# Weight tiles whose high part lies 192 bytes further on, modulo 256, than their low part

## The chip, the core and the metric

One core of a Trainium2 chip runs the program. The metric is the device time of one execution in microseconds; the time before is a median of three runs. TensorE multiplies, VectorE (DVE), ScalarE (ACT) and GpSimd (POOL) prepare operands and take results away, and DMA queues bring the weights in from HBM.

## The reference

A decoder trunk of two layers on 512 tokens of width 1024, in float32. Each layer has a SwiGLU network at half weight, a token mixer (retention in the first layer, forgetting attention in the second), a second SwiGLU network, and a gated per-layer input:

```python
h = h + 0.5 * swiglu(rmsnorm(h, nw[0]), ffn_w_in[i, 0], ffn_w_out[i, 0])
hn = rmsnorm(h, nw[1])
h = h + retention(hn, ...)            # layer 0; forgetting_attention in layer 1
h = h + 0.5 * swiglu(rmsnorm(h, nw[2]), ffn_w_in[i, 1], ffn_w_out[i, 1])
gate = jax.nn.sigmoid(rmsnorm(h, nw[3]) @ ple_w_gate[i])
h = h + gate * (p[i] @ ple_w_proj[i])
```

The inner width of the four SwiGLU networks is 2816. A final RMSNorm ends the trunk.

## The kernel before

All work is on tiles of 128 partitions. Activations are kept transposed: a `unit` is a tile of 128 features by 512 tokens, 2048 bytes in each partition.

**High and low parts.** Every operand of a matmul is kept as two float32r numbers, a rounded high part and the low rest. `split` makes them: ScalarE casts the raw tile into the high part (L83), and VectorE or GpSimd subtracts the high part from the raw tile for the low one (L84). In some stages GpSimd's queue adds the raw tile to its negative by an accumulating DMA instead (`negated`, L125 to L127). A product is then three matmuls: high weights with high activations, high weights with low activations, low weights with high activations. So two matmuls in three load a slice of the high part, 128 columns or 512 bytes of it, as the stationary operand.

**Weights.** `Weights` holds one list of 1024-column sources in the order in which TensorE uses them. `chunk`, `first` and `emit_parts` take a tile `wraw` for the DMA and a tile `w8` (shown as `w` in the profile) of 8192 bytes for the two parts: the high part in its first half, the low part in its second. The pool has three such tiles. In the last stage the pool is replaced by another of five (`wkept`), which also lies elsewhere.

**SwiGLU networks.** The first two blocks of the inner width are done by `plain` (L543), in matmuls of 256 columns of activations, in the order high-high, high-low, low-high. The other 20 blocks of each network go by a scheme of seven products per block (`one`, `two`, `three`), each `product` (L508) being twelve matmuls of 256 columns: first eight with the high part of the weights, each slice twice, then four with the low part. Two of the seven take their weights from the pool's tile; the other five from sums of weights that VectorE makes in tiles of the network's own pool (`s12`, `s34`, shown as `s`, and `a12`, shown as `a`). The second matrix is applied in three pieces by `out_blocks`, through `mm3` (L323 to L325) with 512 columns of activations.

**Mixers and gates.** `proj`, `out_part` and `OutBoth` use `mm3` with 512 columns as well; `v_part` (L702 to L704) has the activations stationary and 512 columns of the weights moving. The first layer's gate (`ple`) runs on 512 columns; the second's, the last stage, in two halves of 256, partly from the five kept tiles.

**Order.** TensorE's instructions run in the order written; the other engines' order is a scheduler's. A tile's wait for its reader (a DMA for a free `wraw`, ScalarE for a free `w`) follows from the pools' sizes.

**Places.** The allocation of the built program gives each tile's first byte in its partition. Units begin at 34,336 and then every 2048 bytes, `wraw` at 124,448, `w` at 140,832, 149,024 and 157,216: all leave 32 when divided by 256. Behind them come `tmp` and the small tiles of `stat`; the latter add 192 modulo 256, so that the networks' `sums`, `s` and `a12`, and the last stage's kept `w`, begin at 184,032 and leave 224. Slices are multiples of 512 bytes, and the halves of a unit 1024 bytes apart, so a slice leaves what its tile does; the low parts lie 2048, 4096 or 8192 bytes behind the high ones and leave the same as them.

Of the kernel before, what the change touches and what calls it, by code (L numbers as in the profile page):

```python
# [12 lines left out]
F32R = mybir.dt.float32r  # L13
# [4 lines left out]
P = 128  # L18
# [36 lines left out]
class Weights:  # L55
# [18 lines left out]
    def load(self, src):  # L74
        raw = self.raw_pool.tile([P, 1024], F32, name="wraw")
        self.nc.sync.dma_start(out=raw[:, : src.shape[1]], in_=src)
        return raw

    def split(self, raw, hi, lo, src=None):
        if self.low is None and src is not None:  # L80
            self.negated(raw, hi, lo, src)
            return
        self.nc.scalar.copy(hi, raw)  # L83
        self.low.tensor_tensor(out=lo, in0=raw, in1=hi.bitcast(F32), op=ALU.subtract)  # L84

    def chunk(self, src):
        n = src.shape[1]
        raw = self.load(src)
        if id(src) in self.placed:
            hi, lo = (t.rearrange("p a c -> p (a c)") for t in self.placed.pop(id(src))())  # L90
            self.split(raw, hi, lo)
            return hi, lo
        if self.spare:
            tiles = [self.spare.pop(0)() for _ in range(4)]
            for i in range(2):
                self.split(raw[:, 512 * i : 512 * (i + 1)], tiles[i], tiles[2 + i])
            return Halves(tiles[0:2]), Halves(tiles[2:4])
        t = self.pool.tile([P, 2, 1024], F32R, name="w8")
        self.split(raw[:, :n], t[:, 0, :n], t[:, 1, :n], src)
        return t[:, 0, :], t[:, 1, :]  # L100

    def emit_parts(self, parts):

        nc = self.nc
        halves = lambda ap: ap.rearrange("p (h c) -> p h c", h=2)
        tiles = [
            (
                self.raw_pool.tile([P, 1024], F32, name="wraw"),
                self.pool.tile([P, 2, 1024], F32R, name="w8"),
            )  # L110
            for _ in range(2)
        ]
        for j0, j1 in parts:
            cs = slice(j0 * P, j1 * P)
            for src, (raw, t) in zip(self.plan, tiles):
                r, hi, lo = (halves(x)[:, :, cs] for x in (raw, t[:, 0, :], t[:, 1, :]))
                nc.sync.dma_start(out=r, in_=halves(src)[:, :, cs])
                nc.vector.tensor_copy(hi, r)
                nc.vector.tensor_tensor(out=lo, in0=r, in1=hi.bitcast(F32), op=ALU.subtract)
            yield  # L120
        self.ready += [(t[:, 0, :], t[:, 1, :]) for _, t in tiles]

    def negated(self, raw, hi, lo, src):

# [4 lines left out]
    def first(self, pair):  # L129

        pair.raw = self.load(pair.q)
        pair.t = self.pool.tile([P, 2, 1024], F32R, name="w8")
        hi, lo = pair.t[:, 0, :], pair.t[:, 1, :]
        if pair.direct:
            self.split(pair.raw, hi, lo)
        else:
            self.negated(pair.raw, hi, lo, pair.q)
# [61 lines left out]
def trunk(ctx, tc, a):  # L199
# [110 lines left out]
    def split(src, hi, lo, scale=None):  # L310

        if scale is None:
            high = nc.scalar.copy(hi, src)
            low = nc.vector.tensor_tensor(out=lo, in0=src, in1=hi.bitcast(F32), op=ALU.subtract)  # L314
        else:
            high = nc.scalar.activation(hi, src, AF.Identity, scale=scale)
            low = nc.vector.scalar_tensor_tensor(
                out=lo, in0=src, scalar=scale, in1=hi.bitcast(F32), op0=ALU.mult, op1=ALU.subtract
            )
        return high, low  # L320

    def mm3(out, wh, wl, xh, xl, first, last):
        nc.tensor.matmul(out, wh, xh, start=first, stop=False)  # L323
        nc.tensor.matmul(out, wh, xl, start=False, stop=False)  # L324
        nc.tensor.matmul(out, wl, xh, start=False, stop=last)  # L325

    def halved(acc):
        hi, lo = temp(F32R), temp(F32R)
        split(acc, hi, lo)
        return hi, lo  # L330
# [13 lines left out]
    class Norm:  # L344
# [9 lines left out]
        def halves(self, b):  # L354
            if self.forms is not None:
                return self.quarters(b)
            hi, lo = self.unit(), self.unit()
            split(h[b], hi, lo, self.gain[:, b : b + 1])
            self.hi.append(hi)
            self.lo.append(lo)  # L360

        def plain(self, b):

            g = self.gain[:, b : b + 1]
            if b % 2:
                hi, lo = self.unit(), self.unit()
                split(h[b], hi, lo, g)
                both = [(hi[:, c], lo[:, c]) for c in HALVES]
            else:
                both = []  # L370
                for i, c in enumerate(HALVES):
                    u = self.unit() if i == 0 else unit(ud)
                    both.append(tuple(u[:, d] for d in HALVES))
                    split(h[b][:, c], *both[i], g)
            n = 1 + b % 2
            if n == 1:
                self.forms.append({})
            self.forms[b // 2].update({f"b{n}1": both[0], f"b{n}2": both[1]})
# [126 lines left out]
    def product(out, w, c, forms, name, first=False):  # L505

        xs = [form[name] for form in forms]
        add = lambda w, x, start, stop: nc.tensor.matmul(  # L508
            out, w, x, start=start, stop=stop, skip_group_check=True
        )  # L510
        for j, (xh, xl) in enumerate(xs):
            wh = w[:, 0, c + j * P : c + (j + 1) * P]
            add(wh, xh, first and j == 0, False)
            add(wh, xl, False, False)
        for j, (xh, xl) in enumerate(xs):
            add(w[:, 1, c + j * P : c + (j + 1) * P], xh, False, j == 3)

    def ffn(i, n, nxt, stack, apool, meanwhile=None):

# [32 lines left out]
        def one(m):  # L552
            pair, g, u = live[m]
            product(g[:, c0], pair.t, 0, n.forms, "b11", True)
            product(g[:, c1], pair.s[0], 0, n.forms, "t1")

        def two(m):
            pair, g, u = live[m]
            product(u[:, c1], pair.s[1], 0, n.forms, "t2", True)
            cc = temp()  # L560
            nc.scalar.copy(cc, g)
            nc.vector.tensor_tensor(out=u[:, c1], in0=u[:, c1], in1=cc[:, c0], op=ALU.add)
            u2 = temp()[:, c0]
            nc.scalar.copy(u2, u[:, c1])
            nc.vector.tensor_tensor(out=g[:, c1], in0=g[:, c1], in1=u2, op=ALU.add)  # L565
            live[m] += (cc,)
# [96 lines left out]
    class OutBoth:  # L663
# [5 lines left out]
        def add(self, i, m):  # L669
            srcs, yhi, ylo = self.parts[i]  # L670
            if (i, m // 2) not in self.ws:
                self.ws[i, m // 2] = W.take(srcs[m // 2])
            wh, wl = self.ws[i, m // 2]
            for k in range(4):
                ks = slice((4 * (m % 2) + k) * P, (4 * (m % 2) + k + 1) * P)
                mm3(self.banks[m], wh[:, ks], wl[:, ks], yhi[k], ylo[k], i == 0 and k == 0, i == 1 and k == 3)
# [560 lines left out]
    norms[4].early = True  # L1237
    first = W.emit_parts(((0, 1), (1, 2), (2, 4)))
    next(first)
    load_x(1, 2)  # L1240
    load_x(2, 4)
# [132 lines left out]
```

## Time and profile before

| | |
|---|---|
| median of three runs (lowest to highest) | 2192.59 us (2189.26 to 2194.67) |
| the profiled execution | 2193.35 us |
| its span, first to last instruction | 2191.5 us |
| instructions | 34,456, of them 13,525 matmuls |
| TensorE busy, weight loads busy | 2142.5 us (98%), 1927.9 us (88%) |
| VectorE, ScalarE, GpSimd busy | 1454.5, 1202.4, 472.6 us |
| read from HBM | 262.71 MB, 121 GB/s over the span |
| granted TensorE clock, mean | 0.994 |

In the profile's rows, PE is TensorE's matmul, PEld its weight load, which runs beside the matmul ahead of it. A group's row has line, engine, operation, output and inputs by name, the shapes and the count, then the group's busy time in microseconds, the mean nanoseconds of one, and the idle time ahead of it with what ended it. A timeline row begins with the start and the length in microseconds; neighbours that are alike are merged, with their count. A matmul's recorded length includes its way through the array, so the cost of one in a stream is the distance from its start to the next one's start.

### The profile page before, as it was taken

To read this page: it belongs to the slowest core of one execution; us is meant where nothing else is said; L and a number is where in the kernel's file an instruction comes from. 1 tells how busy PE (TensorE), PEld (TensorE's weight loads), DVE (VectorE), ACT (ScalarE), POOL (GpSimd) and SP (SyncE) were. 2 spreads that over 40 slices of the span, in tenths; PEclk is the share of its full clock that TensorE was granted. 3 is DMA by queue.
4 is the path that set the end of the run, shared out by engine and by line. 5 is a ranking of instruction groups with operands and counts; after the bars stand their busy time and mean duration, and the time that the engine had idled before them with its cause. 6 is when DMAs were issued, how large, how long until landed. Compare 5 with 4: busy or idle time off the path is not lost.

```text
span 2191.5 us, 34456 instructions
## 1 busy us (share of the span) xinstructions
PE 2142.5 (98%) x13525; PEld 1927.9 (88%) x13525; DVE 1454.5 (66%) x2629; ACT 1202.4 (55%) x2027; POOL 472.6 (22%) x354
## 2 busy tenths in 40 slices
PE   8999999999999999999998999999999999999997
PEld 7999997888888798989988999898788899999987
DVE  8686766352533677767758687775675696777765
ACT  7465553433333574745556556464787774655544
POOL 0010003444344000101142011012334200100055
PEclk9999999999999999999999999999999999999999
DMA  5465562222222244746523555463622144654631
GB/s 174 124 167 148 140 164 97 82 95 77 94 77 87 77 128 132 177 119 152 144 94 97 129 160 149 137 167 105 152 81 88 67 125 114 161 154 139 155 106 40
DMA packets 85315, 267.08 MB, mean 122 GB/s; under 512 B 9360, under 2 KB 12944, under 8 KB 85152
## 3 DMA queue, kind: packets, MB, share of 16 engines
q1 hardware_dynamic: 63328, 209.78, 28.2%
q0 software_dynamic: 20592, 54.01, 14.6%
q8 instruction: 106, 1.74, 0.3%
q10 hardware_dynamic: 1232, 1.09, 0.1%
q14 instruction: 57, 0.47, 0.1%
HBM read 262.71 MB, written 2.13 MB: 121 GB/s over the span
## 4 chain that ended last, share of the span: by engine, by line
PE 85%; DVE 6%; ACT 4%; DMA 2%; issue 2%; POOL 1%; SPq 0%; ACTq 0%; DVEq 0%; POOLq 0%
PE bank L508 33%; PE bank L325 14%; PE bank L323 14%; PE bank L324 13%; PE bank L543 4%; PE bank L703 2%; PE bank L702 2%; PE bank L704 2%; DMA wraw<-in_ffn_w_in 1%; ACT p L1006 1%; DVE w L84 1%; ACT p L1008 1%; ACT w L83 1%; DVE tlo L314 1%; PE bank L337 0%
## 5 line engine op out<-in xcount | busy, mean ns | idle before, releaser
L83 ACT CAST w<-wraw 128x1024 fp32r<-128x1024 f32 (+1 forms) x240 | 243.4, 1021 | 420.0 <-PE bank L325 254.9
L325 PE MATMUL bank<-unit_a,w 128*128 128x512 f32 x736 | 287.2, 390 | 4.3 <-DVE w L84 2.6
L323 PE MATMUL bank<-unit_a,w 128*128 128x512 f32 x736 | 288.5, 392 | 1.9 <-ACT w L83 1.6
L324 PE MATMUL bank<-unit_a,w 128*128 128x512 f32 x736 | 286.7, 390 | 0.2 <-DVE unit_a L314 0.2
L84 POOL TENSOR_TENSOR w<-wraw,w 128x1024 fp32r<-128x1024 f32 x93 | 226.8, 2442 | 259.3 <-ACT w L83 246.8
L83 ACT CAST s<-sums 128x512 fp32r<-128x512 f32 x320 | 191.8, 617 | 153.4 <-DVE sums L157 107.4
L325 PE MATMUL bank<-unit_d,w 128*128 128x512 f32 (+1 forms) x712 | 268.2, 377 | 4.6 <-DVE w L84 4.6
L323 PE MATMUL bank<-unit_d,w 128*128 128x512 f32 (+1 forms) x712 | 269.3, 378 | 3.2 <-ACT w L83 1.6
L324 PE MATMUL bank<-unit_d,w 128*128 128x512 f32 (+1 forms) x712 | 268.0, 376 | 1.8 <-DVE unit_d L314 1.8
L84 DVE TENSOR_TENSOR s<-sums,s 128x512 fp32r<-128x512 f32 x320 | 214.1, 685 | 75.8 <-ACT s L83 75.3
L127 POOL DMA_DIRECT2D a<-in_ffn_w_in x80 | 70.3, 878 | 643.4 <-ACT a L126 422.0
L84 DVE TENSOR_TENSOR w<-wraw,w 128x1024 fp32r<-128x1024 f32 (+1 forms) x147 | 173.3, 1184 | 19.5 <-ACT w L83 19.3
L508 PE MATMUL bank<-unit_b,s 128*128 128x256 f32 x880 | 184.4, 276 | 0.7 <-DVE bank L565 0.7
L508 PE MATMUL bank<-unit_d,s 128*128 128x256 f32 x1140 | 178.4, 276 | 0.0
L508 PE MATMUL bank<-unit_a,s 128*128 128x256 f32 x1260 | 175.0, 276 | 1.4 <-ACT unit_a L387 0.9
L604 DVE SCALAR_TENSOR_TENSOR tmp<-bank,rows 128x512 f32<-128x512 f32 x96 | 66.0, 689 | 164.9 <-PE bank L325 163.7
L325 PEld LDWEIGHTS bank<-unit_a,w 128*128 128x128 f32 x736 | 138.1, 188 | 35.5 <-DVE w L84 4.3
L323 PEld LDWEIGHTS bank<-unit_a,w 128*128 128x128 f32 x736 | 138.2, 188 | 32.2 <-ACT w L83 3.5
L324 PEld LDWEIGHTS bank<-unit_a,w 128*128 128x128 f32 x736 | 138.2, 188 | 28.5 <-DVE unit_a L314 0.5
L325 PEld LDWEIGHTS bank<-unit_d,w 128*128 128x128 f32 x712 | 134.3, 189 | 30.7 <-DVE w L84 6.6
L323 PEld LDWEIGHTS bank<-unit_d,w 128*128 128x128 f32 x712 | 134.4, 189 | 30.2 <-ACT w L83 3.3
L508 PEld LDWEIGHTS bank<-unit_a,s 128*128 128x128 f32 x1260 | 158.0, 188 | 1.8 <-ACT unit_a L387 1.1
(292 smaller groups left out, 4787.9 us busy)
## 6 DMA issues: line engine op xcount, KB each, us to landing
wraw<-in_ffn_w_in SPq DMA_DIRECT2D x174, 512.0 KB, 4.3
wraw<-in_ffn_w_out SPq DMA_DIRECT2D x64, 512.0 KB, 4.7
w<-in_ffn_w_in POOLq DMA_DIRECT2D x56, 512.0 KB, 5.4
a<-in_ffn_w_in POOLq DMA_DIRECT2D x80, 256.0 KB, 6.3
wraw<-in_ffn_w_out SPq DMA_DIRECT2D x32, 384.0 KB, 3.7
wraw<-in_ret_qk SPq DMA_DIRECT2D x16, 512.0 KB, 3.5
wraw<-in_ret_v SPq DMA_DIRECT2D x16, 512.0 KB, 3.6
wraw<-in_ret_g SPq DMA_DIRECT2D x16, 512.0 KB, 3.5
```

Of the source, the lines that this page charges most:

```text
L83: self.nc.scalar.copy(hi, raw)
L84: self.low.tensor_tensor(out=lo, in0=raw, in1=hi.bitcast(F32), op=ALU.subtract)
L127: self.nc.gpsimd.dma_start(out=lo, in_=src, accum_op=ALU.add)
L323: nc.tensor.matmul(out, wh, xh, start=first, stop=False)
L324: nc.tensor.matmul(out, wh, xl, start=False, stop=False)
L325: nc.tensor.matmul(out, wl, xh, start=False, stop=last)
L508: add = lambda w, x, start, stop: nc.tensor.matmul(out, w, x, start=start, stop=stop, skip_group_check=True)
L543: nc.tensor.matmul(o[:, HALVES[t]], x[:, ks], y, start=k == t == q == 0, stop=k == KB - 1 and q == 2, skip_group_check=True,)
L604: nc.vector.scalar_tensor_tensor(out=t1, in0=o, scalar=-0.5, in1=n.r, op0=ALU.mult, op1=ALU.mult)
L702: nc.tensor.matmul(os[t], xh, wh[:, js], start=k == 0, stop=False)
L703: nc.tensor.matmul(os[t], xh, wl[:, js], start=False, stop=False)
L704: nc.tensor.matmul(os[t], xl, wh[:, js], start=False, stop=k == KB - 1)
```

## The change

All tiles of the weight pool come from one function. It makes them 2112 elements long, 8448 bytes, which is 256 more; the high part begins 192 bytes into the tile, the low part 4352 bytes into it, a multiple of 256. The high part therefore leaves 224 modulo 256 and the low part 32. In the last stage's kept tiles, which begin at 224, the high part leaves 160 and the low part 224. The three tiles together are 768 bytes longer, so that all that lies behind them keeps what it leaves modulo 256. The users of the tile take the two parts as a pair in place of a three-dimensional tile; `product` accepts both. No instruction, DMA or wait is added or removed.

```diff
+    def wide(self, src):
+
+        at = 48
+        t = self.pool.tile([P, 2112], F32R, name="w8")
+        return t[:, at : at + 1024], t[:, at + 1040 :]
+
...
-        t = self.pool.tile([P, 2, 1024], F32R, name="w8")
-        self.split(raw[:, :n], t[:, 0, :n], t[:, 1, :n], src)
-        return t[:, 0, :], t[:, 1, :]
+        hi, lo = self.wide(src)
+        self.split(raw[:, :n], hi[:, :n], lo[:, :n], src)
+        return hi, lo
...
-                self.pool.tile([P, 2, 1024], F32R, name="w8"),
+                *self.wide(src),
...
-        pair.t = self.pool.tile([P, 2, 1024], F32R, name="w8")
-        hi, lo = pair.t[:, 0, :], pair.t[:, 1, :]
+        pair.t = hi, lo = self.wide(pair.q)
...
+        both = w if isinstance(w, tuple) else (w[:, 0, :], w[:, 1, :])
...
-            wh = w[:, 0, c + j * P : c + (j + 1) * P]
+            wh = both[0][:, c + j * P : c + (j + 1) * P]
...
-            add(w[:, 1, c + j * P : c + (j + 1) * P], xh, False, j == 3)
+            add(both[1][:, c + j * P : c + (j + 1) * P], xh, False, j == 3)
```

More of the change, by code (lines that the diff above doesn't have):

```diff
@@ L108, in emit_parts @@
                 self.raw_pool.tile([P, 1024], F32, name="wraw"),
-                self.pool.tile([P, 2, 1024], F32R, name="w8"),
+                *self.wide(src),
             )
-            for _ in range(2)
+            for src in self.plan[:2]
         ]
@@ L114, in emit_parts @@
             cs = slice(j0 * P, j1 * P)
-            for src, (raw, t) in zip(self.plan, tiles):
-                r, hi, lo = (halves(x)[:, :, cs] for x in (raw, t[:, 0, :], t[:, 1, :]))
+            for src, (raw, wh, wl) in zip(self.plan, tiles):
+                r, hi, lo = (halves(x)[:, :, cs] for x in (raw, wh, wl))
                 nc.sync.dma_start(out=r, in_=halves(src)[:, :, cs])
@@ L120, in emit_parts @@
             yield
-        self.ready += [(t[:, 0, :], t[:, 1, :]) for _, t in tiles]
+        self.ready += [(wh, wl) for _, wh, wl in tiles]
     def negated(self, raw, hi, lo, src):
```

## The prediction, made before the change was run

> **What bounds the kernel now.** I read the page first (busy times, chain), then the groups of TensorE by shape, then TensorE's own timeline in four stretches, because the change moves bytes and nothing else.
>
> ```profile
> span 2191.5 us, 34456 instructions
> PE 2142.5 (98%) x13525; PEld 1927.9 (88%) x13525; DVE 1454.5 (66%) x2629; ACT 1202.4 (55%) x2027; POOL 472.6 (22%) x354
> PE 85%; DVE 6%; ACT 4%; DMA 2%; issue 2%; POOL 1%; SPq 0%; ACTq 0%; DVEq 0%; POOLq 0%
> ```
>
> TensorE is busy for 98% of the span and carries 85% of the chain that ended last. So a nanosecond on each matmul is what counts, and a slot of another engine is not. The groups by shape (mean ns of one is the last figure ahead of the second bar):
>
> ```profile
> L323 PE MATMUL bank<-unit_a,w 128*128 128x512 f32 x736 | 288.5, 392 | 1.9 <-ACT w L83 1.6 <-DVE tmp L1040 0.3
> L323 PE MATMUL bank<-unit_d,w 128*128 128x512 f32 x616 | 241.9, 393 | 3.2 <-ACT w L83 1.6 <-DVE unit_b L317 0.6 <-ACT unit_d L313 0.5
> L508 PE MATMUL bank<-unit_a,s 128*128 128x256 f32 x1260 | 175.0, 276 | 1.4 <-ACT unit_a L387 0.9 <-DVE unit_a L388 0.4
> L508 PE MATMUL bank<-unit_b,w 128*128 128x256 f32 x720 | 132.1, 283 | 0.4 <-ACT tmp L564 0.3
> L508 PE MATMUL bank<-unit_a,w 128*128 128x256 f32 x540 | 80.3, 283 | 1.7 <-ACT tmp L564 1.7
> L323 PEld LDWEIGHTS bank<-unit_a,w 128*128 128x128 f32 x736 | 138.2, 188 | 32.2 <-ACT w L83 3.5
> ```
>
> One product, one shape, two prices: 283 ns with weights from `w`, 276 from `s`. The two kinds of tile differ in place. By the allocation, the units and `w` begin at bytes that leave 32 modulo 256, `s`, `sums` and `a12` at 224, since the small tiles of `stat` between them add 192. The timeline has what counts, start to start:
>
> ```profile
> 138.27 1.52 PE L508 MATMUL bank<-unit_a,s 128*128 128x256 f32 x12
> 139.63 0.73 PE L508 MATMUL bank<-unit_b,a 128*128 128x256 f32 x5
> ...
> 140.99 0.88 PE L508 MATMUL bank<-unit_b,w 128*128 128x256 f32 x6
> ...
> 142.43 0.39 PE L508 MATMUL bank<-unit_a,s 128*128 128x256 f32 x2
> ```
>
> Twelve products from `s` take 139.63-138.27 = 1.36 us, 113.3 ns each; twelve from `w` 142.43-140.99 = 1.44 us, 120.0 ns. So 6.7 ns go where weights and moving operand sit equally modulo 256. The wide matmuls, all on `w` at 32:
>
> ```profile
> 1165.11 0.39 PE L323 MATMUL bank<-unit_a,w 128*128 128x512 f32 x1
> ...
> 1168.96 0.39 PE L325 MATMUL bank<-unit_c,w 128*128 128x512 f32 x1
> 1169.18 0.75 PE L543 MATMUL bank<-unit_b,s 128*128 128x256 f32 x5
> ...
> 1171.66 0.52 PE L543 MATMUL bank<-unit_d,s 128*128 128x256 f32 x3
> ```
>
> The seventeen steps of the first pair give 3.85/17 = 226.5 ns, twice 113.3: for 512 columns it streams as fast, per column, as the good case for 256. The second pair is a warning. It is a `plain` block whose weights lie in `s` tiles, at 224, straight after a wide stretch: 21 matmuls in 2.48 us, 118.1 ns, not 113.3. Place alone does not settle the price; how one got there counts too. The last stage, where five `w` tiles are in a pool of their own at 224, has both:
>
> ```profile
> 2138.60 0.28 PE L323 MATMUL bank<-unit_d,w 128*128 128x256 f32 x1
> ...
> 2140.37 0.28 PE L323 MATMUL bank<-unit_c,w 128*128 128x256 f32 x1
> 2163.43 0.28 PE L323 MATMUL bank<-unit_d,w 128*128 128x256 f32 x1
> ...
> 2165.02 0.28 PE L325 MATMUL bank<-unit_d,w 128*128 128x256 f32 x1
> ```
>
> 15 steps in 1.77 us are 118.0 ns; 14 in 1.59 are 113.6, and that stretch directly follows matmuls with weights at 32. I call these the bad and the good state of weights at 224.
>
> **The change, part by part.** Instructions, DMAs, queues and waits stay as they are. The three tiles grow by 768 bytes together, three times 256, so nothing behind them moves modulo 256. The high part goes from 32 to 224; the low part stays at 32. In the kept pool, high goes from 224 to 160, low stays at 224.
>
> (a) *Products from `w`* (L508): 4 networks x 20 blocks x 2 products x 12 = 1920, of which 8 in 12 load the high part: 1280 x 6.7 = 8.5 us less. Bounds: the full 8.5, or, in the bad state, 1280 x 2.0 = 2.6. I take the good one, for in each block these products stand among `s` products, which run in it.
>
> (b) *`plain` and the narrow gates.* Two loads in three are high.
>
> ```profile
> L543 PE MATMUL bank<-unit_b,w 128*128 128x256 f32 x220 | 35.6, 302 | 3.0 <-DVE w L84 1.4 <-DVE w L119 1.1 <-DVE unit_b L317 0.4
> L543 PE MATMUL bank<-unit_d,w 128*128 128x256 f32 x204 | 30.7, 297 | 0.0
> L543 PE MATMUL bank<-unit_a,w 128*128 128x256 f32 x144 | 20.4, 284 | 0.0
> L543 PE MATMUL bank<-unit_c,w 128*128 128x256 f32 x104 | 16.4, 287 | 0.0
> ```
>
> 672 matmuls, 448 high: between 448 x 2.0 = 0.9 us (as at 1169 us, the same line) and 3.0. Nearest is the same line's 118.1, with a low part at 32 in every third, which favours the good state: I take 2.0 us. The gates' kept tiles go to 160, which no row shows: some 160 matmuls at 113.3 to 120, from 1.1 us more to 0.7 less. I take nothing.
>
> (c) *Wide matmuls* (L323 to L325): 736+616 = 1352 triples, 2704 with high weights, and six calls of 96 in `v_part`, where `w` moves and the units are loaded. No row has wide matmuls with weights at 224. Below: 6.7 ns less each, 18.1 us. Above: 4.7 more (118.0-113.3) on all 4056, 19.1 us. I take zero: a load is recorded with 188 ns and has 226.5 to hide in against 113.3, and 226.5 is already the good rate per column. `v_part` likewise zero, within 576 x 4.7 = 2.7 either way.
>
> (d) *Writers.* ScalarE, VectorE and GpSimd write or read the high part at its new place. VectorE pays 684 ns where its inputs lie at 224 and 32, and 686 where both lie at 32:
>
> ```profile
> L157 DVE TENSOR_TENSOR sums<-wraw 128x512 f32<-128x512 f32 x160 | 109.6, 686 | 55.7 <-DMA wraw<-in_ffn_w_in 55.3
> L157 DVE TENSOR_TENSOR sums<-sums,wraw 128x512 f32<-128x512 f32 x160 | 109.4, 684 | 0.8
> L84 POOL TENSOR_TENSOR w<-wraw,w 128x1024 fp32r<-128x1024 f32 x93 | 226.8, 2442 | 259.3 <-ACT w L83 246.8 <-issue 11.9
> L84 POOL TENSOR_TENSOR s<-wraw,s 128x1024 fp32r<-128x1024 f32 x1 | 2.9, 2886 | 0.0
> ```
>
> A subtraction of GpSimd with its high part at 224 took 2886 ns against a mean of 2442 at 32. If that is the place, 93 x 0.44 = 41 us more on an engine that is idle 78% of the span. I cost it at nothing; with that cover gone it would show as TensorE waiting for `w` L84 on POOL.
>
> Sum: 8.5+2.0 = 10.5 us less on TensorE, which is idle only 49 us; the next engine is at 66%, so I let it through in full. The profiled execution took 2193.35 us (span 2191.5, 1.85 around it), 0.8 above the median of the runs, 2192.59. It becomes 2182.9, and the median 2182.1.
>
> **The Trainium skill beside the rows.** 6.7 ns between two places of the same operand, above, are not what the Trainium skill says ("TensorE: Matmul & The Clock Gate", section "Step-by-step: what each phase is for"): by it, weight loads and the moving operand have independent read ports and loading the next weights takes no read bandwidth from the running matmul. By that rule the sum would be nought, 2192.6; the trace disagrees by 6.7 ns in 120. The same page ("Back-to-back issue gap") puts isolated matmuls at columns/2.4 + 2.5 ns, 215.8 for 512. The trace has 226.5; by the page 10.7 ns could still go from each wide matmul, an estimate of 29 us over the 2704, which speaks for rival 2.
>
> **Rivals.** (1) *Wide matmuls pay* (the other side). After `s` products the wide stretch does not start at its good rate:
>
> ```profile
> 87.47 0.40 PE L323 MATMUL bank<-unit_d,w 128*128 128x512 f32 x1
> ...
> 88.63 0.39 PE L325 MATMUL bank<-unit_d,w 128*128 128x512 f32 x1
> ...
> 90.44 0.39 PE L324 MATMUL bank<-unit_d,w 128*128 128x512 f32 x1
> ```
>
> The first five take 232 ns (1.16/5), the next eight 226.3 (1.81/8): loads and stream slide into step, at one fixed place of the weights. With the place changing at each high, high, low, they may never get into step. At 4.7 ns on all 4056 wide matmuls that is 19.1 us against 10.5: 2201. It decides from 2.6 ns a matmul (10.5 us) on. For it: the bad state at 1169 us comes straight from a wide stretch in step. Against: slack for the load.
>
> (2) *Wide matmuls gain too.* If 6.7 ns are hidden in 226.5 as they are in 120.0, 18.1 more go: 2164. Against: 226.5 is exactly two good halves.
>
> (3) *The products fall into the bad state.* Now twelve matmuls at 32 bring them into the good one; after the change only four low ones in a row do. At 118 the 1920 products from `w` gain 3.8, the 80 blocks x 60 from `s` and `a12` lose 4800 x 4.7 = 22.6: 2211.
>
> (4) *Nothing to see*: high and low loads must both move for the price to fall, 2192.6. Against: at 140.99 and at 142.43 the price goes with the matmul's own weights at once, whatever its neighbours have.
>
> (5) *Half*: (a) and (b) at their lower bounds, 3.5 us: 2189.
>
> **How the numbers follow.** My sum 0.32; rival 1 0.26; rival 2 0.10; rival 3 0.14; rival 4 0.08; half 0.10. Forecast 2182. 0.3%, 6.6 us, is about what a measurement of this kernel tells from no change: faster is my sum and rival 2, 0.42; same is rivals 4 and 5 and the part of rival 1 below 4.2 ns a matmul, 0.27; slower is the rest of rival 1 and rival 3, 0.31. The range, 2164 to 2212, takes in rivals 1 and 2 and the start of 3; what lies above is 3 with 1 together. My own sum's range is 2178 to 2187.
>
> **What would show it.** L508 on `w`: eight starts 113 ns apart, then four of 119 to 121; group means between 276 and 283. L323 to L325 at 226 to 227 ns in step means (c) is right; 230 or more means rival 1; 220 rival 2. `s` products at 118 mean rival 3. POOL L84 at 2.9 us with TensorE idle for it would break (d). I am wrong if the step between loads and stream is set by more than the place of the matmul's own weights.

## The result, and the profile after

The changed kernel takes 2217.32 us (median of 4 runs, 2216.07 to 2218.01) against 2191.10 us for the kernel before beside it (4 runs, 2189.26 to 2194.67). The ratio is 1.0115, with an interval of 1.0099 to 1.0131. That is 26 us slower, where 10 us faster was forecast. The profiled execution took 2218.01 us, at a granted clock of 0.995 (0.994 before).

First the page of the changed kernel: the span, the busy times and the chain that ended last.

```profile
span 2216.2 us, 34456 instructions
PE 2169.2 (98%) x13525; PEld 1943.3 (88%) x13525; DVE 1457.0 (66%) x2629; ACT 1202.4 (54%) x2027; POOL 472.5 (21%) x354
PE 86%; DVE 7%; ACT 4%; issue 2%; DMA 2%; POOL 0%; SPq 0%; DVEq 0%; ACTq 0%; POOLq 0%
```

The span grew by 24.7 us and TensorE's busy time by 26.7, with the same 13,525 matmuls. VectorE, ScalarE and GpSimd moved by 2.5 us at most. So the time is not in the other engines: the matmuls themselves became dearer, as the steps below show. Next the groups of the changed kernel. Lines of code were added, so the line that was L508 is now L514, L323 is L328, L543 is L549, L702 is L708 and L84 is L90. The last row is `v_part` before the change.

```profile
L514 PE MATMUL bank<-unit_a,s 128*128 128x256 f32 x1260 | 180.4, 279 | 1.3 <-ACT unit_a L392 0.9 <-DVE unit_a L393 0.4
L514 PE MATMUL bank<-unit_b,w 128*128 128x256 f32 x720 | 130.6, 280 | 0.0
L328 PE MATMUL bank<-unit_a,w 128*128 128x512 f32 x736 | 291.7, 396 | 1.8 <-ACT w L89 1.6 <-DVE tmp L1046 0.3
L708 PE MATMUL bank<-w,unit_a 128*128 128x512 f32 x128 | 50.9, 398 | 0.0
L549 PE MATMUL bank<-unit_d,w 128*128 128x256 f32 x204 | 28.7, 285 | 0.0
L90 POOL TENSOR_TENSOR w<-wraw,w 128x1024 fp32r<-128x1024 f32 x93 | 227.0, 2444 | 267.2 <-ACT w L89 250.6
```

```profile
L702 PE MATMUL bank<-w,unit_a 128*128 128x512 f32 x128 | 49.9, 390 | 0.0
```

The figure to read is the mean ahead of the second bar. Products from `w` fell from 283 to 280, and the `plain` group of `unit_d` from 297 to 285. But products from `s`, whose tiles were not touched, rose from 276 to 279, wide matmuls from 392 to 396 and `v_part` from 390 to 398. GpSimd's subtraction stayed at 2444 ns (2442 before).

The timeline has the steps. Columns are start, length, engine, line, operation and count.

```profile
138.52 1.58 PE L514 MATMUL bank<-unit_a,s 128*128 128x256 f32 x12
139.93 0.75 PE L514 MATMUL bank<-unit_b,a 128*128 128x256 f32 x5
...
141.35 0.87 PE L514 MATMUL bank<-unit_b,w 128*128 128x256 f32 x6
...
142.76 2.99 PE L514 MATMUL bank<-unit_a,s 128*128 128x256 f32 x24
145.59 1.59 PE L514 MATMUL bank<-unit_a,w 128*128 128x256 f32 x12
```

Twelve matmuls with weights from `s` take 139.93-138.52 = 1.41 us, 117.5 ns each; before they took 113.3. Twelve from `w` take 142.76-141.35 = 1.41 us as well, where they took 1.44. The next 24 from `s` take 2.83 us, 117.9 ns each: this is the bad state, and it does not end. Wide matmuls and `v_part`:

```profile
1169.76 0.39 PE L328 MATMUL bank<-unit_c,w 128*128 128x512 f32 x1
...
1184.64 0.39 PE L330 MATMUL bank<-unit_c,w 128*128 128x512 f32 x1
```

```profile
393.55 0.40 PE L709 MATMUL bank<-w,unit_a 128*128 128x512 f32 x1
...
395.89 0.40 PE L710 MATMUL bank<-w,unit_a 128*128 128x512 f32 x1
```

Between the two wide rows lie 65 steps: 14.88/65 = 228.9 ns, late in a long stretch, where 226.6 stood before. In `v_part` ten steps take 2.34 us, 234 ns; over the whole kernel before, its mean step was 227.0.

Taking every start in both traces and adding up the steps shorter than 300 ns by kind of matmul (waits are the longer ones) gives the account of the change:

```
kind of matmul          steps    mean before -> after    total
products from s, a12    4796     113.45 -> 117.82 ns     +21.0 us
wide, weights from w    4033     227.23 -> 229.45        + 9.0
v_part                   572     227.02 -> 234.18        + 4.1
products from w         1919     120.11 -> 118.42        - 3.2
plain                    753     127.6  -> 124.8         - 1.9
narrow gates             381     120.6  -> 118.6         - 0.8
```

The sum is 28.2 us. Steps of 300 ns and more, which hold the waits, came to 93.2 us before and 89.0 after, so some 4 us come back; that TensorE, being later, has less to wait for is the likely reason. That leaves about the 24.7 us of the span.

### The profile page after: what moved, and what is told of

Its sections match the earlier page's. It is cut to its first block, busy times and chain, and to the rows that moved or that the text cites. A ratio compares the mean times of both kernels' runs of the same rounds, so it can differ in the third digit from the quotient of the medians.

```text
span 2216.2 us, 34456 instructions
## 1 busy us (share of the span) xinstructions
PE 2169.2 (98%) x13525; PEld 1943.3 (88%) x13525; DVE 1457.0 (66%) x2629; ACT 1202.4 (54%) x2027; POOL 472.5 (21%) x354
## 4 chain that ended last, share of the span: by engine, by line
PE 86%; DVE 7%; ACT 4%; issue 2%; DMA 2%; POOL 0%; SPq 0%; DVEq 0%; ACTq 0%; POOLq 0%
PE bank L514 34%; PE bank L330 14%; PE bank L328 14%; PE bank L329 14%; PE bank L549 3%; PE bank L709 2%; PE bank L708 2%; PE bank L710 2%; DMA wraw<-in_ffn_w_in 1%; DVE w L90 1%; ACT p L1012 1%; ACT w L89 1%; DVE tlo L319 1%; ACT p L1014 1%; PE bank L342 0%
## 5 line engine op out<-in xcount | busy, mean ns | idle before, releaser
L328 PE MATMUL bank<-unit_a,w 128*128 128x512 f32 x736 | 291.7, 396 | 1.8 <-ACT w L89 1.6
L90 POOL TENSOR_TENSOR w<-wraw,w 128x1024 fp32r<-128x1024 f32 x93 | 227.0, 2444 | 267.2 <-ACT w L89 250.6
L328 PE MATMUL bank<-unit_d,w 128*128 128x512 f32 (+1 forms) x712 | 270.7, 380 | 3.3 <-ACT w L89 1.6
L90 DVE TENSOR_TENSOR s<-sums,s 128x512 fp32r<-128x512 f32 x320 | 214.8, 686 | 80.7 <-ACT s L89 80.0
L514 PE MATMUL bank<-unit_b,s 128*128 128x256 f32 x880 | 187.6, 279 | 0.7 <-DVE bank L571 0.7
L90 DVE TENSOR_TENSOR w<-wraw,w 128x1024 fp32r<-128x1024 f32 (+1 forms) x147 | 173.4, 1185 | 17.1 <-ACT w L89 17.0
L514 PE MATMUL bank<-unit_d,s 128*128 128x256 f32 x1140 | 183.3, 279 | 0.0
L514 PE MATMUL bank<-unit_a,s 128*128 128x256 f32 x1260 | 180.4, 279 | 1.3 <-ACT unit_a L392 0.9
L328 PEld LDWEIGHTS bank<-unit_a,w 128*128 128x128 f32 x736 | 138.7, 188 | 33.6 <-ACT w L89 3.5
L514 PEld LDWEIGHTS bank<-unit_a,s 128*128 128x128 f32 x1260 | 162.5, 188 | 1.7 <-ACT unit_a L392 1.1
L328 PEld LDWEIGHTS bank<-unit_d,w 128*128 128x128 f32 x712 | 133.8, 188 | 31.0 <-ACT w L89 3.2
```

Of the source, the lines that this page charges most:

```text
L514: add = lambda w, x, start, stop: nc.tensor.matmul(out, w, x, start=start, stop=stop, skip_group_check=True)
```

## The experiments

Two theories stood against each other. "In step": what a matmul costs depends on whether the loading of the next weights and the moving stream have slid into a common rhythm; the places modulo 256 decide which rhythms exist, and the order of the places decides which one is reached. "Place alone": each matmul has a price by its own weights' place.

### The places by themselves

A kernel of 71 separate streams of matmuls with all other engines silent; it leaves out the whole computation of the reference. Places are given as the bytes that the weights lie beyond the moving units, modulo 256; 192 in these streams is 224 in the kernel, and 0 is 32. High/low stands for the two parts.

```diff
+for width in (256, 512):
+    SECTIONS += [[(width, "mm3", h, l, 32)] for h in R for l in R]
+SECTIONS += [[(256, "product", h, l, 8)] for h in R for l in R]
...
+G, B = (256, "product", 0, 0, 2), (512, "mm3", 0, 0, 8)
...
+    one, s = (256, "product", h, l, 1), lambda n: (256, "product", 192, 192, n)
+    SECTIONS += [[B, one, s(2), one, s(3), one, s(2), one, s(3), one, s(2), one, s(3)]]
```

Each bracket is (columns, order, place of the high part, place of the low part, count): B is a wide stretch at 0, G two products at 0, `one` a block with the places of `w`, and `s` blocks at 192.

> Leaves out the whole computation: 71 separate streams of 96 to 288 matmuls on one tile of units (at 32 modulo 256) and one tile of weights, each stream started from a stop, with the weights' high and low slices 0, 64, 128 or 192 bytes further on modulo 256 than the units, in the order high, high, low or in the order of a product (eight high, four low), at 256 or 512 columns. Theory 'in step' (the cost of a matmul hangs on whether loads and moving operand have slid into step, and only a long run at one place lets them): 256 columns at 192 from a stop stay near 118 ns, the same after 24 matmuls at 0 run at 113; 512 columns at 0 settle at 226.7, mixed places (192 with 0) stay at 229 to 231. Rival 'place alone' (each matmul pays by the place of its own weights, whatever came ahead): 192 costs the same from a stop as after a run at 0, and a mixed stream the mean of the two constant ones. Other engines are silent here; if mixed streams at 512 columns run at 226.7, the loss in the kernel comes from them and both fall.

The steady step in nanoseconds, from the starts in each stream, in the order high, high, low from a stop:

```
256 columns           low 0   64    128   192
            high   0  120.0  117.8  119.1  117.8
                  64  117.8  113.3  118.3  113.3
                 128  118.3  120.0  118.7  120.0
                 192  117.8  118.9  115.6  117.8
512 columns        0  226.7  231.1  231.1  231.1
                  64  233.3  233.3  231.1  231.8
                 128  233.3  230.0  232.4  233.3
                 192  228.9  233.3  231.1  228.9
```

For 512 columns only 0/0, the place of before, settles at 226.7; 192/0, the place of after, settles at 228.9, which is what the kernel shows. The timeline of these streams has one row for each (96 matmuls each in the first two rows, 276 in the others):

```profile
221.28 22.05 PE L56 MATMUL bank<-u,w 128*128 128x512 f32 x96 [0.51 <-DVE sink L60]
...
497.46 22.28 PE L56 MATMUL bank<-u,w 128*128 128x512 f32 x96 [0.51 <-DVE sink L60]
...
1125.14 34.77 PE L56 MATMUL bank<-u,w 128*128 128x512 f32 x276 [0.51 <-DVE sink L60]
1160.42 35.45 PE L56 MATMUL bank<-u,w 128*128 128x512 f32 x276 [0.51 <-DVE sink L60]
1196.38 34.63 PE L56 MATMUL bank<-u,w 128*128 128x512 f32 x276 [0.51 <-DVE sink L60]
```

The first two are 0/0 and 192/0 at 512 columns: 0.23 us over 96 matmuls is 2.4 ns each. The other three are the network in small: a wide stretch, then blocks w, s, s, w, s, s, s three times over, with w at 0/0, 192/0 and 0/192. With w at 0/0 the 180 matmuls at 192 run at 113.3 ns; with w at 192/0 they run at 117.8 from beginning to end, 0.8 us more, of which the cheaper w gives 0.1 back; with w at 0/192 they are at 113.3 again. The `s` weights lie at the same place in all three. No writer, DMA or other engine runs beside them, so contention with those is out as the source of these steps.

In the product order, weights at 192/192 ran at 117.8 ns from a stop and after a wide stretch, and at 113.3 after two products at 0. Weights at 192/0 have two lasting prices as well: 118.4 ns after the wide stretch and 115.5 after two products at 0. Each price is kept for all 96 matmuls. "Place alone" falls with that.

### One half of the change each

In the first kernel only the tiles of the networks' pairs (which feed the products) have high at 224, in the second only all other tiles (wide matmuls, `v_part`, `plain`, gates). Parts that don't move lie at 32; all tiles have the changed length.

```diff
+        pairs = any(isinstance(p, Pair) and p.q is src for p in self.plan)
+        hi, lo = (192, 0) if pairs else (0, 0)      # first kernel
+        hi, lo = (0, 0) if pairs else (192, 0)      # second kernel
```

> Only the tiles for the networks' products have their high part at 224; all others have both parts at 32, in tiles of the changed length. 'In step': wide matmuls and v_part back at 227, so 13 us come back (9.0 and 4.1 by the sums of their steps), the products stay in the bad state at 118 since four low ones are too short a run at 32: 2204. Rival 'the wide stretch brings it in' (products are bad only since the mixed wide stretch ahead never gets in step): s back at 113.3, all of the loss gone and 8 us gained: 2183.

Measured: 2202.87 us against 2190.34, ratio 1.0057 (1.0042 to 1.0072). Groups of this kernel (lines one further on):

```profile
L515 PE MATMUL bank<-unit_a,s 128*128 128x256 f32 x1260 | 179.9, 280 | 1.4 <-ACT unit_a L393 1.0 <-DVE unit_a L394 0.4
L515 PE MATMUL bank<-unit_a,w 128*128 128x256 f32 x540 | 79.3, 281 | 1.6 <-ACT tmp L571 1.6
L329 PE MATMUL bank<-unit_a,w 128*128 128x512 f32 x736 | 288.7, 392 | 1.9 <-ACT w L90 1.6 <-DVE tmp L1047 0.3
```

> The reverse: the products' tiles have both parts at 32, all others the high part at 224. 'In step': the products' twelve at 32 bring s to 113.3 again (21 us back), wide matmuls at 229 to 230 and v_part at 234 stay: 2191 + 13 - 3 for the plain blocks and narrow gates = 2201. Rival 'the wide stretch brings it in': s stays near 118, 2215 or more.

Measured: 2200.65 us, ratio 1.0044 (1.0027 to 1.0061). Its groups:

```profile
L515 PE MATMUL bank<-unit_a,s 128*128 128x256 f32 x1260 | 175.1, 277 | 1.4 <-ACT unit_a L393 1.0 <-DVE unit_a L394 0.4
L515 PE MATMUL bank<-unit_a,w 128*128 128x256 f32 x540 | 80.4, 284 | 2.0 <-ACT tmp L571 2.0
L329 PE MATMUL bank<-unit_a,w 128*128 128x512 f32 x736 | 291.9, 397 | 1.8 <-ACT w L90 1.5 <-DVE tmp L1047 0.3
L710 PE MATMUL bank<-w,unit_a 128*128 128x512 f32 x128 | 51.0, 399 | 0.0
```

Both came out as "in step" said (2204 and 2201). With the pairs moved, `s` stands at 280 and wide at 392; with the others moved, `s` is at 277, wide at 397 and `v_part` at 399. So wide matmuls at 192/0 do not cost `s` its state as long as the pairs' blocks lie at 0/0; with the pairs moved it is lost in most places though the wide matmuls run as before. The two differences, 12.5 and 10.3 us, add up to 22.8 of the 26.2. The steps of `s` show the rest: 117.07 ns in the first kernel and 117.82 in the full change, 0.75 x 4796 = 3.6 us. Products come in twelve long stretches, three in each network. In the first kernel three of them keep `s` at 113.3 to their end, with `w` at 115.6; each begins straight after a `plain` block with both parts at 0. The other nine, behind wide stretches or at the start of the kernel, settle at 117.8, and in the full change all twelve do. So blocks at 192/0 do not break the good state: they cannot bring it in.

### Both parts at 224

```diff
+        hi, lo = (192, 192) if pairs else (192, 192)
```

> Both parts of every tile of the pool 192 bytes further on, so that a stream has one place throughout. 'In step': wide matmuls settle, at 226.7 if 192 can get in step at all, at 231 if not (18 us); products never pass 32 and stay at 118 throughout, 19 us more: 2210, or 2228. Rival 'place alone': all products at 113.3, 2180 with the wide ones unchanged.

Measured: 2209.74 us, ratio 1.0088 (1.0066 to 1.0109). Wide steps are 229.35 ns and `v_part` 233.35, close to the full change. Products from `s` and from `w` are both at 116.1, a mixture: four of the twelve stretches run at 113.3 (one of them only until near its end), the other eight at 117.8. The wide stretches ahead of them step by 226, 229 and 232 ns in turn; the four good ones follow a last step of 231 or 232, the four others that a wide stretch precedes one of 226 or 229. That the expected 2210 was met is luck: it stood for wide matmuls at 226.7 and products at 118 throughout, and neither came true. Instead wide matmuls and `v_part` cost 8.5 and 3.6 us more than before, `s` 12.7 more and `w` 7.7 less. That all weights lie at one place is therefore not enough: at 192/192 no wide stretch, here or in the streams, came to 226.7, and products ran in either state by how they were entered.

### What brings it in

Streams again, the computation left out.

```diff
+for k in (1, 2, 3, 4, 6, 8, 10, 12):
+    SECTIONS += [[B, (256, "one", 0, 0, k), W(192, 192, 4)]]
+for k in (1, 2, 3, 4, 6, 8, 10, 12):
+    SECTIONS += [[B, W(192, 192, 2), (256, "one", 0, 0, k), W(192, 192, 4)]]
...
+        SECTIONS += [[entry, W(h, l), S1(2), W(h, l), S1(3), W(h, l), S1(2), (512, "mm3", 0, 0, 16)]]
...
+    SECTIONS += [[(512, "swap", e, e, 32)]]    # the units loaded, the tile moving
```

> Separate streams of 128x256 and 128x512 matmuls, as in the first set of streams; the whole computation of the reference is left out. Places are bytes that the weights lie beyond the moving operand, modulo 256. (1) Eight wide triples at 0, then k matmuls of 256 columns at 0 (k = 1, 2, 3, 4, 6, 8, 10, 12), then 48 at 192; and the same with 24 at 192 ahead of the k. Theory 'in step': the state at 192 is chosen by what ran before it, and a run at 0 must be long enough to bring it in: 117.8 ns at 192 after k up to 4, 113.3 after 8 and more, the change somewhere between. Rival 'the last one decides': 113.3 from k = 1. Rival 'the whole past decides (wide stretch)': 117.8 at every k. (2) Blocks w, s, s, w, s, s, s with w at 64/64 and others, s at 192 or 64, after a wide stretch and after products at 0: by theory 64/64 is at 113.3 whatever came before, and s at 64 too; what s at 192 does after w at 64 is open: 113.3 if a run at 64 brings it in as a run at 0 does, 117.8 if not. (3) A wide stretch at 0 after blocks at 192 and 64: in step at 226.7 after five to ten matmuls. (4) 512 columns moving from the tile at 0, 64, 128, 192 with the units loaded as weights, as in the value projection: if the distance between the two counts, 226.7 at 0 and some 233 at 192 (which is weights 64 beyond the moving operand); if the loaded operand's own place counts, 226.7 throughout.

Out of the bad state, k matmuls at 0 bring 192 into the good one from k = 8 on: 117.8 ns after 1, 2, 3, 4 and 6, 113.3 after 8, 10 and 12. Two rows of the timeline, k = 6 and k = 8:

```profile
187.60 14.93 PE L67 MATMUL bank<-u,w 128*128 128x512 f32 x102 [0.51 <-DVE sink L71]
203.04 14.95 PE L67 MATMUL bank<-u,w 128*128 128x512 f32 x104 [0.51 <-DVE sink L71]
```

Two matmuls more, 0.24 us at their own price, and the stream is only 0.02 us longer, since the 48 behind them fall from 117.8 to 113.3. Straight from a wide stretch in step fewer do: 1 did, 2 did not, 3 and more did. So, with `s` at 192, a block of `w` at 0/0, twelve in a row, brings it in; one at 192/0, with four in a row, does not bring it in from the bad state, and one at 0/192, with eight, does. That is the cause of the 21 us: before the change each block of a network had two such runs of twelve, and after it no run is longer than four.

The units as weights and the tile moving at 0, 64, 128 and 192 gave 226.7, 228.9, 233.3 and 233.3 ns over the last 24 steps. A moving operand at 192 has its weights 64 beyond it, and weights at 64 ran at 233.3 above; at 64 its weights are 192 beyond it, and they ran at 228.9. At 128 the distance is the same either way, and 233.3 stands against 232.4 above. The distance between the two operands counts, to about 1 ns, not the place of one of them. `v_part` is of this kind: two of its three matmuls move the high part, at 224, past units at 32, and it runs at 234 ns.

Part (2) of the expectation was wrong: w at 64/64, which ran at 113.3 from a stop, ran at 117.8 after a wide stretch and after products at 0, and stayed there when `s` was at 64 too. Two places that differ did better. From the second block of w on, 64/64 with `s` at 192 ran at 113.3, and 192/64 with `s` at 192 or at 64 did so from the first or second block on. A count of matmuls at 0 is not the whole rule: with w at 0/64, eight at 0 in each block, `s` at 192 stayed at 117.7, and with w at 64/0, four at 0, it ran at 113.3. Part (3) came true: behind the blocks, wide matmuls at 0 were back at 226.7 after five to nine steps.

### The low part at 224, the high part at 32

```diff
+        hi, lo = (0, 192) if pairs else (0, 0)
```

> In the tiles of the networks' pairs the high part stays at 32 modulo 256, as before the change, and the low part goes to 224; all other tiles have both at 32. Theory 'in step' (the first set of streams had this order at 120 for the eight high matmuls, 113.3 for the four low ones and 113.3 for s): 640 low matmuls x 6.7 ns = 4.3 us less than before, 2186 to 2187. Rival 'any part of the pairs at 224 keeps s in the bad state': 4800 x 4.5 = 21.6 more and 640 x 2.2 = 1.4 less, 2211.

Measured: 2188.81 us against 2191.93, ratio 0.9986 (0.9977 to 0.9994). Products from `w` fell from 120.11 to 117.91 ns, 4.2 us, and `s` stayed at 113.45. The same tile with its parts the other way round thus gains a little where the change lost. The two places and the tile's length are those of the change; what differs is that the run at 0 is eight long in place of four.

### A gap and nothing else

The kernel before, with 128 bytes ahead of the networks' pool. No instruction differs and no tile has its parts at different places.

```diff
     stat = ctx.enter_context(tc.tile_pool(name="stat", bufs=1))
+    stat.tile([P, 32], F32, name="gap")
```

> The kernel before with a gap of 128 bytes ahead of the networks' own pool: sums, s, a12 and the last kept tiles at 96 modulo 256 (64 beyond the units) instead of 224, every pool tile at 32 as before. No instruction differs. Theory (block sequence 0/0 with s at 64 in the second set of streams: s 117.8 throughout, w 119.7): 4800 x 4.3 = 20.6 us more: 2212. Rival 'the change cost time because two parts of one tile lie differently': 2192, since no tile does here.

Measured: 2211.18 us against 2190.69, ratio 1.0087 (1.0073 to 1.0100), +20.5 us. A group and the timeline of this kernel:

```profile
L509 PE MATMUL bank<-unit_a,s 128*128 128x256 f32 x1260 | 180.7, 281 | 1.3 <-ACT unit_a L388 0.9 <-DVE unit_a L389 0.4
```

```profile
138.52 1.58 PE L509 MATMUL bank<-unit_a,s 128*128 128x256 f32 x12
139.93 0.75 PE L509 MATMUL bank<-unit_b,a 128*128 128x256 f32 x5
```

The twelve from `s` take 1.41 us, exactly as after the change. Over the kernel they are at 117.88 ns, 4.43 x 4797 = 21.2 us, and `w` is at 119.8. By the Trainium skill ("TensorE: Matmul & The Clock Gate", section "Step-by-step: what each phase is for") loading weights takes no read bandwidth from the running matmul; by that rule 128 bytes between two pools cost nothing, and the measurement disagrees by 4.4 ns on each of these matmuls.

### Four layouts that should gain

```diff
+        hi, lo = (64, 64) if pairs else (0, 0)                  # pairs at 96 modulo 256
...
+    stat.tile([P, 32], F32, name="gap")                         # second kernel: s at 96 as well
...
+        if pairs:                                               # third and fourth: high 224, low 96
+            return t[:, 1072:2096], t[:, 16:1040]
```

> Both parts of the pairs' tiles at 96 modulo 256 (64 beyond the units), all other tiles at 32, s and a12 at 224 as before. In the first set of streams 64/64 was the one place that ran at 113.33 ns from a stop. Theory: the 1920 products from w go from 120.0 to 113.3, 12.8 us less, plain some 3 less, wide matmuls unchanged. Then s decides: 2175 if products at 64 bring s at 224 into its good state, 2197 if s stands at 117.8 for the lack of a run at 32 (4800 x 4.5 = 21.6 more). Rival 'only 32 against 224 is special': w unchanged, 2191.

Measured: 2183.31 us, ratio 0.9961 (0.9949 to 0.9973). Products from `w` are at 114.08 ns, 11.6 us less, and `s` is at 113.74, 1.4 us more. The rest of the 2175 was a slip: `plain` does not use the pairs' tiles in this kernel and stayed at 120.

> As the kernel with the pairs at 64 beyond the units, and a gap of 128 bytes ahead of the networks' own pool, so that sums, s, a12 and the kept tiles lie at 96 modulo 256 too instead of 224. Theory: everything of 256 columns in the networks runs at 113.3 whatever came before: 12.8 us less on w, some 3 on plain, s as before, wide unchanged: 2175, and not 2197. Rival 'no fixed place is good by itself': s or w at 118, 2185 to 2213.

Measured: 2206.43 us, ratio 1.0064 (1.0052 to 1.0076), against 2175 expected. `s` stands at 117.48 ns, `w` at 117.57: the bad state at one common place, as the second set of streams shows it. The rival named there, that no fixed place is good by itself, was right.

> Pairs' tiles with the high part at 224 modulo 256 (192 beyond the units) and the low part at 96 (64 beyond); all other tiles at 32, s and a12 at 224 as before. In the second set of streams the block sequence with w at 192/64 and s at 192 ran at 113.3 throughout, from its first or second product on, whatever came before. Theory: w 120.0 to 113.4 (1920 x 6.6 = 12.7 us less), s as before at 113.4, nothing else: 2179, 4 below the kernel with the pairs at 64/64. Rival from the result of the change, 'eight high loads at 224 spoil s': s at 117.5, 2199.

Measured: 2182.49 us against 2190.69, ratio 0.9956 (0.9941 to 0.9971). Its timeline:

```profile
139.01 0.84 PE L516 MATMUL bank<-unit_b,w 128*128 128x256 f32 x6
...
140.37 2.88 PE L516 MATMUL bank<-unit_a,s 128*128 128x256 f32 x24
...
143.09 1.52 PE L516 MATMUL bank<-unit_a,w 128*128 128x256 f32 x12
144.45 0.73 PE L516 MATMUL bank<-unit_b,s 128*128 128x256 f32 x5
```

Twelve from `w`, twenty-four from `s` and twelve from `w` again: 5.44 us for 48, 113.3 ns each. That is the state that the prediction counted on, with the high part at the very place that the change gave it, 224; the low part at 96 in place of 32 makes the difference. It is not reached everywhere: the first of the twelve stretches, behind `plain` at the start of the kernel, settled at 117.8. The 4 us expected below the kernel with 64/64 did not show either (ratios 0.9956 and 0.9961).

> As the one before, and the tiles of the plain blocks with the high part at 96 and the low part at 224 (64/192: in the first set of streams that place ran at 113.3 in the order high, high, low, after some eight matmuls). Theory: 672 matmuls from 120 to 113.3 at best, 4.5 us less, and not below 1 us (118.5): 2175 to 2178. Rival: plain always starts from a stop and stays out of step at 117.8 to 120: 2178 to 2179.

Here the `plain` tiles are moved as well:

```diff
+        if id(src) in self.plain:
+            return t[:, 16:1040], t[:, 1072:2096]
```

Measured: 2180.56 us, ratio 0.9949 (0.9933 to 0.9965). The steps of `plain` fell by 4.9 us, from the 95.9 of the kernel before to 91.0, its median from 120 to 114, so `plain` does not always stay out of step. The time against the kernel ahead of it differs by less than the intervals, and the 2175 to 2178 expected were not reached: steps of 300 ns and more came to 98.3 us in that kernel and 103.6 here, against 93.2 before the change, so part of what the matmuls gain goes into waits. It is the fastest measured here: 0.5% under the kernel before, 1.7% under the changed one.

## Why the prediction was wrong, point by point

The forecast was 2182 us with a range to 2212; the result was 2217. Rivals 1 and 3 came true together, the one case that the range left out above.

(a) *Products from `w`: failed, and with it the largest term.* The prediction took the good state "for in each block these products stand among `s` products, which run in it". That had cause and effect the wrong way round: `s` ran in the good state because twelve matmuls at 32 came by in each block. What the runs showed in its place: with four low matmuls at 32 in a row the good state is not brought in, `s` goes from 113.45 to 117.82 ns (21.0 us more), and `w` stops at 118.42 (3.2 us less in place of 8.5). Rival 3 said so, and its sum was nearly right: 22.6 us lost on `s` and 3.8 gained on `w`. It had a chance of 0.14. The evidence for it was in the prediction already, in the `plain` block that runs at 118.1 straight after a wide stretch.

(b) *`plain` and the gates: about right in size, not in working.* 2.0 and nothing were forecast; 1.9 and 0.8 us were gained. The good state that the low part at 32 was to favour is not where the gain comes from: the steps of `plain` from `w` went from a median of 120 to one of 118, and 76 of 661 fell below 115. That the sum fits is partly luck.

(c) *Wide matmuls: failed.* The slack of a 188 ns load in 226.5 was taken as cover. But 226.7 ns is itself the in-step rhythm, and of the sixteen pairs of places in the streams only 0/0 settles there. Rival 1 had the direction, but only in part the mechanism: it put the loss down to the place changing at each high, high, low, and 192/192, where no place changes, settles at the same 228.9. Its price was too high as well: 2.2 ns in place of 4.7. `v_part` was bounded at 4.7 ns; it lost 7.2, beyond the bound, which came from 256-column rows.

(d) *Writers: right.* GpSimd's subtraction, its high part at 224, took 2444 ns against 2442. With both parts at 224 it took 2466, so the places do not explain the 2886 of one instruction; what does stays open.

The wrong sum, -10.5, and the right one, +28 less some 4 of shorter waits, differ by two states and not by a size. The guess in the last line of "what would show it", that the step between loads and stream might be set by more than the place of the matmul's own weights, is what the runs showed.

The other rule of the Trainium skill that the prediction weighed ("Back-to-back issue gap" of the same page, 215.8 ns for 512 columns as an estimate) spoke for rival 2, a further gain on wide matmuls. No place of the streams goes below 226.67, so no run here shows it.

## What to carry to other kernels

Where TensorE is the bound and its matmuls follow each other without waits, read the distance from start to start, not the length, and set it beside the addresses of both operands modulo 256: 128 bytes ahead of one pool cost 0.9% here with no instruction changed. Before a place is changed, ask which matmuls bring the others into their good rhythm; a term taken from a neighbour's rate holds only if the neighbour keeps it. A stream of a few hundred matmuls with the places of the plan and the same order, blocks and entry included, gave the state of `s` that the kernel then showed in the layouts that were run both ways; streams from a stop alone misled here.

## What was not expected of the hardware

- The price of a 256-column matmul depends on the history: the same tiles in the same order keep 113.3 or 117.8 ns (products from `s`), and 115.5 or 118.4 (192/0), for as long as the order goes on. Eight matmuls at 0 left the bad state of 192/192; six did not.
- The distance of the loaded operand from the moving one counts, whichever of them is the tile: 228.9 ns at 192, 233.3 at 64, 226.7 at 0, for 512 columns.
- Mixed places can be better than one: for 256 columns, 192/64 and 64/192 with `s` at 192 ran at 113.3 ns, everything at 64 or everything at 192 at 117.8 after a wide stretch at 0.
- What in the chip the two operands share stays open; the runs show the rhythms, not their cause. Why two matmuls at 0 failed where one and three sufficed, straight from a wide stretch, wasn't followed up.
